# Wider moving operands in a two-block transformer kernel, and another order of its first loads

## The chip, the cores and the metric

The kernel runs on one core of a Trainium2 chip. The metric is the device time of one execution in microseconds; the kernel before takes 840.6 us (median of 3 runs, 839.73 to 841.76).

## What is computed

A sequence of 256 tokens with 1024 channels passes through two blocks in fp32. The parts that matter here:

```python
x = first_block(x, ...)      # even layer (mLSTM + sparse attention), odd layer (gated recurrence)
x = second_block(x, c, ...)  # 2 layers, each: a mixer, then a squared-ReLU MLP

def even_layer(h, w_in, b_in, ...):      # h = rms_norm(x, norm_w[0])
    proj = h @ w_in + b_in               # q, k, v, gates ...
def hgrn2_layer(h, w_in, b_in, ...):     # h = rms_norm(x, norm_w[1])
    fp, iv, qp, z = jnp.split(h @ w_in + b_in, 4, axis=-1)
def sq_relu_mlp(h, w1, w2):              # w1: 1024 x 4096, w2: 4096 x 1024
    return jnp.square(jax.nn.relu(h @ w1)) @ w2
# second_block, layer i
mod = c_act @ ada_w[i] + ada_b[i]        # six 1024-vectors: shifts, scales, gates
x = x + g2[:, None, :] * sq_relu_mlp(modulate(rmsnorm(x, g), sh2, sc2), w1[i], w2[i])
```

## The kernel before, in words

**Numbers.** Each large product is made of fp32r operands in two parts: a value is a rounded high part plus a low rest. A product is the sum of three: high weight by high activation, high weight by low activation, low weight by high activation (L212 to L214 in `mm_T`, L197 to L199 in `tiles_tok`). Each of the three is one TensorE instruction of 128 rows, with its own weight load. Plain fp32 products (norm sums, transposes, attention scores) stand as two records each in the trace.

**Layout.** Activations lie channel-major: 128 channels by 256 tokens, eight such slices. `tile_T` gives 128 output channels: the weight is the loaded operand, the 256 tokens (258 where two columns of the shift are carried along) are streamed. `tiles_tok` gives token-major outputs for v and sv of the even layer and iv of the odd one: 128 tokens of the activation are loaded, 256 columns of the weight are streamed, once for each of the two token halves.

**Weights.** `Weights.piece` loads 1 MB chunks from HBM on SP's queue into three `raw` buffers and splits each half chunk (a piece of 128x1024) by an ACT copy to `whi` (L153) and a DVE subtraction to `wlo` (L154), four buffers each. So a piece costs ACT one cast, DVE one subtraction, and PE 24 products.

**Side work.** The modulation vectors `mod` are formed by DVE (L342) from 96 chunks of 512 KB (`araw`, two buffers, also on SP's queue). A generator hands out this work; `step(n)` places one of its 72 steps (one or two chunks) among other work. SP's queue is in order: an `araw` load that waits for its buffer holds the weight loads behind it.

**Second MLP product.** The 32 slices of the squared ReLU are kept as `ghi` and `glo`, each 128 x 32 x 256. For each of 8 output tiles, 4 pieces of `w2` are taken, and for each of their 8 slices the three products L212 to L214 go into one PSUM bank of 256 columns. `scaled_add` (L321) then adds the tile, times the gate, to `xT`.

**Start.** `prm` (all small parameters, 170 KB, the norm weights among them) is loaded from ACT's queue. SP's queue loads `xT` two slices at a time (256 KB, 2 KB per partition out of rows of 8 KB) and the first weight chunk in three parts (256, 256 and 512 KB, again out of rows of 8 KB), interleaved. `Norm.operand` casts each slice, scaled by the norm weight (ACT L271, DVE L272); `ahead` splits the first piece in two halves; `square` forms the sums for the norm (ACT L277, DVE L280, PE L285). Then the columns of the even layer follow, four tiles before the constants (`cst`, rows) are loaded, the rest after.

The order on each engine is set by a planner that takes the program's order, modelled costs and priorities; PE's order follows the program closely.

Of the kernel before, what the change touches and what calls it, by code (L numbers as in the profile page):

```python
# [8 lines left out]
F32 = mybir.dt.float32  # L9
# [9 lines left out]
T = 256  # L19
# [15 lines left out]
class _Columns:  # L35
# [15 lines left out]
    ("norm_w", 16), ("ev_b", 35), ("f_bias", 1), ("conv_w", 32), ("conv_b", 8),  # L51
# [14 lines left out]
def tile_kernel(ctx: ExitStack, tc: tile.TileContext, io: dict, out: bass.AP):  # L66
# [36 lines left out]
    prm = mk(base, [128, PRM.n], F32, "prm")  # L103
    xT = mk(base, [128, KT, T], F32, "xT")
# [21 lines left out]
    G.memset(ones, 1.0)  # L126
    ident_bf = mk(base, [128, 128], BF16, "identbf")
# [29 lines left out]
    class Weights:  # L157
# [5 lines left out]
        def first(self, c0, c1):  # L163
# [23 lines left out]
    def tiles_tok(w, i, pair, evict):  # L187

        ps = [gbank()[:, :256] for _ in range(2)]
        for half in range(2):  # L190
            wh, wl = w.piece(i + half, 256)
            for tb in range(2):
                ts_ = slice(tb * 128, tb * 128 + 128)
                for k4 in range(4):
                    k = half * 4 + k4
                    st, sp = k == 0, k == KT - 1
                    PE.matmul(ps[tb], pair.hi(k)[:, ts_], wh[:, k4, :], start=st, stop=False)  # L197
                    PE.matmul(ps[tb], pair.lo(k)[:, ts_], wh[:, k4, :], start=False, stop=False)  # L198
                    PE.matmul(ps[tb], pair.hi(k)[:, ts_], wl[:, k4, :], start=False, stop=sp)  # L199
        for tb in range(2):  # L200
            evict(tb, ps[tb])
# [44 lines left out]
    class Norm:  # L246
# [13 lines left out]
        def operand(self, k):  # L260
            if self.pair is None:
                return
            x, p = xT[:, k, :], k // 4
            if self.shift is not None and p not in self.pair.parts:
                hi, lo = [a[:, :, T : T + 2] for a in self.pair.part(p)]
                sh = self.shift[:, 4 * p : 4 * p + 4, None].to_broadcast([128, 4, 2])
                S.copy(hi, sh)
                V.tensor_sub(lo, sh, hi)
            g = self.gain[:, k : k + 1]
            hi, lo = self.pair.hi(k)[:, :T], self.pair.lo(k)[:, :T]  # L270
            S.activation(hi, x, AF.Copy, scale=g)  # L271
            V.scalar_tensor_tensor(lo, x, g, hi, op0=ALU.mult, op1=ALU.subtract)  # L272
# [109 lines left out]
    def even_layer(norm, nxt, w):  # L382
        with ExitStack() as es:
# [13 lines left out]
            V.tensor_tensor(gbias, P("ev_b", b0), P("f_bias"), op=ALU.add)  # L397
            hbias = mk(ev, [128, 35], F32, "hbias")
            V.tensor_scalar(hbias, P("ev_b"), 0.5, None, op0=ALU.mult)
# [51 lines left out]
            def columns(names):  # L451
                for name in names:
                    ti = EV_TILES.index(name)
                    if name in ("v0", "v1", "v2", "v3", "sv0", "sv1"):
                        dst, row = (v, row_v) if name[0] == "v" else (sv, row_sv)
                        c0 = int(name[-1]) * 128
                        if c0 % 256 == 0:
                            tiles_tok(w, ti, pair, lambda tb, ps: V.scalar_tensor_tensor(
                                dst[:, tb, c0 : c0 + 256], ps, rcol[:, tb : tb + 1], row[:, c0 : c0 + 256], op0=ALU.mult, op1=ALU.add))
# [14 lines left out]
            columns(EV_TILES[:4])  # L474
# [5 lines left out]
            columns(EV_TILES[4:11])  # L480
# [296 lines left out]
    def hgrn_layer(norm, nxt):  # L777
        with ExitStack() as es:
# [213 lines left out]
    def mlp(layer, mod, norm, nxt):  # L992
        with ExitStack() as es:
            mp = es.enter_context(tc.tile_pool(name="mp", bufs=1))
            pair = norm.pair
            ghi = mk(mp, [128, 32, T], F32R, "ghi")
            glo = mk(mp, [128, 32, T], F32R, "glo")
            w1 = Weights(lambda c: io["mlp_w1"][layer, c])
            w2 = Weights(lambda c: io["mlp_w2"][layer, c])
            for n in range(32):  # L1000
                if layer == 0 and n % 2 == 0:
                    step(11)
                if layer and n % 4 == 3:
                    step(12)
                if layer == 0 and n == 16:
                    sgu_prepare(*consts)
                ps = gbank()[:, : pair.w]
                tile_T(ps, w1, n, pair)
                r = norm.scaled(ps)
# [4 lines left out]
                S.copy(ghi[:, n, :], r)  # L1014
                V.tensor_sub(glo[:, n, :], r, ghi[:, n, :])
# [110 lines left out]
    n1 = Norm(P("norm_w", 8, 8))  # L1126
# [110 lines left out]
def _pack(inp):  # L1237
# [3 lines left out]
    a["xT"] = np.ascontiguousarray(g["x"][0].T.reshape(KT, 128, T).transpose(1, 0, 2))  # L1241
# [3 lines left out]
    for i, name in enumerate(EV_TILES):  # L1245
        if name not in tok:
            ps.append(_pieces(_take(w, tiles[i]), 8, 128))
        elif name in ("v0", "v2", "sv0"):
            ps.append(_pieces(_take(w, np.concatenate(tiles[i : i + 2])), 4, 256))
    a["ev_w_in"] = _paired(*ps, np.zeros((1, 128, 1024), f))  # L1250
    order = np.concatenate([np.arange(512)] + [512 + np.concatenate([j * 64 + np.arange(64), (j + 4) * 64 + np.arange(64)]) for j in range(4)])
    a["ev_w_out"] = _paired(_pieces(g["ev_w_out"][0][order], 8, 128))
    a["od_w_in"] = _paired(*[_pieces(m, 4 if i == 1 else 8, 256 if i == 1 else 128) for i, m in enumerate(np.split(g["od_w_in"][0], 4, 1))])
# [12 lines left out]
    def per_part(v):  # L1266
# [9 lines left out]
        "norm_w": per_part(g["norm_w"]),  # L1276
# [19 lines left out]
    }  # L1296
    a["prm"] = np.ascontiguousarray(np.concatenate([parts[n].reshape(128, -1) for n in PRM.at], 1))
# [26 lines left out]
```

## Time and profile before

| | |
|---|---|
| median of 3 runs | 840.6 us |
| profiled execution, its own time | 842.29 us |
| its span, first to last instruction | 840.5 us |
| TensorE matmul busy | 810.0 us (96%), 7172 instructions |
| VectorE busy | 667.1 us (79%) |
| ScalarE busy | 516.3 us (61%) |
| DMA | 184.72 MB, mean 220 GB/s |

PE's busy time is the union of overlapping instructions: one 256-column product is shown as 0.28 us, but the next starts 0.12 us after it. What a product takes of PE is the distance between starts, or a window's length divided by the number of products in it.

### The profile page before, as it was taken

Reading aid. Unit: us, or ns where it says so; the run is one execution under the profiler, and the core shown is the slowest. Engines: PE = TensorE matmul, PEld = TensorE weight load, DVE = VectorE, ACT = ScalarE, POOL = GpSimd, SP = SyncE. Lnnn points to the kernel's source line nnn. Section 1 sums busy time; section 2 is a strip of 40 time slices with the busy share of each in tenths; the row PEclk is TensorE's granted clock in tenths of the full one; section 3 lists DMA queues with packets and bytes.
Section 4 is the critical chain, followed back from the end, with each engine's and each line's share of the span. In section 5 each row is a group of like instructions: output and inputs, shape, how many; then the busy total and the mean of one; then the engine's idle time right before and its main releaser. Section 6 shows DMA issues by size and latency. Waiting matters only on the chain.

```text
span 840.5 us, 17614 instructions
## 1 busy us (share of the span) xinstructions
PE 810.0 (96%) x7172; PEld 772.0 (92%) x7172; DVE 667.1 (79%) x1247; ACT 516.3 (61%) x918; POOL 4.9 (1%) x19
## 2 busy tenths in 40 slices
PE   6999999998999999999999998999999999999996
PEld 5989787888998998999999998999999999999995
DVE  7679888899999999999998977756678777754542
ACT  6645656686876565658777633445647777754431
POOL 0000000001000000000000000000000000000000
PEclk9999999999999999999999999999999999999998
DMA  9664266657785777667888888865445454554521
GB/s 328 220 221 171 101 198 218 233 180 265 293 310 201 239 254 282 228 226 246 310 277 289 297 298 295 296 208 194 152 151 185 166 198 161 193 188 168 196 102 50
DMA packets 34497, 184.72 MB, mean 220 GB/s; under 512 B 3825, under 2 KB 4465, under 8 KB 19057
## 3 DMA queue, kind: packets, MB, share of 16 engines
q1 hardware_dynamic: 33984, 182.85, 62.3%
q8 instruction: 56, 0.92, 0.4%
q10 hardware_dynamic: 432, 0.76, 0.3%
q14 instruction: 25, 0.20, 0.1%
HBM read 182.55 MB, written 1.05 MB: 218 GB/s over the span
## 4 chain that ended last, share of the span: by engine, by line
PE 66%; DMA 13%; DVE 10%; ACT 5%; issue 4%; SPq 0%; DVEq 0%; ACTq 0%
PE g L212 17%; PE g L214 17%; PE g L213 16%; DMA araw<-in_ada_w_dram 12%; DVE wlo L154 4%; DVE araw L342 3%; ACT whi L153 1%; PE m L848 1%; PE g L197 1%; PE g L198 1%; PE g L199 1%; PE m L739 1%; PE long L767 1%; PE m L285 1%; DVE nt L301 1%
## 5 line engine op out<-in xcount | busy, mean ns | idle before, releaser
L212 PE MATMUL g<-ahi,whi 128*128 128x258 f32 (+1 forms) x1256 | 359.6, 289 | 10.9 <-ACT whi L153 6.7
L214 PE MATMUL g<-ahi,wlo 128*128 128x258 f32 (+1 forms) x1256 | 356.6, 285 | 3.1 <-DVE wlo L154 3.1
L213 PE MATMUL g<-alo,whi 128*128 128x258 f32 (+1 forms) x1256 | 357.7, 286 | 0.1
L153 ACT CAST whi<-raw 128x1024 fp32r<-128x1024 f32 (+1 forms) x238 | 246.6, 1043 | 168.2 <-PE g L213 134.1
L154 DVE TENSOR_TENSOR wlo<-raw,whi 128x1024 fp32r<-128x1024 f32 (+1 forms) x238 | 289.2, 1217 | 73.7 <-ACT whi L153 73.2
L212 PEld LDWEIGHTS g<-ahi,whi 128*128 128x128 f32 x1256 | 238.3, 190 | 15.6 <-ACT whi L153 6.9
L214 PEld LDWEIGHTS g<-ahi,wlo 128*128 128x128 f32 x1256 | 238.9, 190 | 5.3 <-DVE wlo L154 4.3
L213 PEld LDWEIGHTS g<-alo,whi 128*128 128x128 f32 x1256 | 239.5, 191 | 2.6 <-issue 1.2
L214 PE MATMUL g<-ghi,wlo 128*128 128x256 f32 x512 | 144.5, 282 | 4.5 <-DVE wlo L154 4.4
L213 PE MATMUL g<-glo,whi 128*128 128x256 f32 x512 | 144.7, 283 | 0.0
L212 PE MATMUL g<-ghi,whi 128*128 128x256 f32 x512 | 144.7, 283 | 0.0
L342 DVE CUSTOM_DVE_ANT_0 araw<-araw,row_c,prm 128x1024 f32<-128x1024 f32 x96 | 122.6, 1280 | 25.8 <-DMA araw<-in_ada_w_dram 25.6
L214 PEld LDWEIGHTS g<-ghi,wlo 128*128 128x128 f32 x512 | 96.9, 189 | 5.8 <-DVE wlo L154 5.8
L213 PEld LDWEIGHTS g<-glo,whi 128*128 128x128 f32 x512 | 96.4, 188 | 0.1
L212 PEld LDWEIGHTS g<-ghi,whi 128*128 128x128 f32 x512 | 96.0, 187 | 0.0
L301 DVE TENSOR_TENSOR nt<-g,nrstd 128x256 f32<-128x256 f32 x133 | 55.6, 420 | 21.7 <-PE g L214 21.6
L1012 ACT ACTIVATE nt<-nt,nb 128x256 f32<-128x256 f32 x64 | 32.3, 507 | 19.5 <-DVE nb L1011 19.5
L271 ACT ACTIVATE ahi<-xT,gains 128x256 fp32r<-128x256 f32 x32 | 16.2, 506 | 38.7 <-DVE xT L321 38.0
L197 PE MATMUL g<-whi,ahi 128*128 128x256 f32 x112 | 32.7, 292 | 0.0
L198 PE MATMUL g<-whi,alo 128*128 128x256 f32 x112 | 32.0, 286 | 0.0
L199 PE MATMUL g<-wlo,ahi 128*128 128x256 f32 x112 | 32.0, 286 | 0.0
L277 ACT ACTIVATE sq<-xT 128x256 f32<-128x256 f32 x56 | 22.5, 404 | 12.0 <-DVE xT L321 10.9
(288 smaller groups left out, 824.8 us busy)
## 6 DMA issues: line engine op xcount, KB each, us to landing
raw<-in_mlp_w_dram SPq DMA_DIRECT2D x64, 1024.0 KB, 4.9
araw<-in_ada_w_dram SPq DMA_DIRECT2D x96, 512.0 KB, 5.1
raw<-in_ev_w_in_dram SPq DMA_DIRECT2D x17, 1024.0 KB, 5.4
raw<-in_od_w_in_dram SPq DMA_DIRECT2D x16, 1024.0 KB, 5.6
raw<-in_sgu_w_in_dram SPq DMA_DIRECT2D x8, 1024.0 KB, 4.7
raw<-in_ev_w_out_dram SPq DMA_DIRECT2D x4, 1024.0 KB, 4.9
raw<-in_od_w_out_dram SPq DMA_DIRECT2D x4, 1024.0 KB, 6.0
raw<-in_sgu_w_out_dram SPq DMA_DIRECT2D x4, 1024.0 KB, 4.8
```

Of the source, the lines that this page charges most:

```text
L153: S.copy(hi[:, c], r[:, c])
L154: V.tensor_sub(lo[:, c], r[:, c], hi[:, c])
L197: PE.matmul(ps[tb], pair.hi(k)[:, ts_], wh[:, k4, :], start=st, stop=False)
L198: PE.matmul(ps[tb], pair.lo(k)[:, ts_], wh[:, k4, :], start=False, stop=False)
L199: PE.matmul(ps[tb], pair.hi(k)[:, ts_], wl[:, k4, :], start=False, stop=sp)
L212: PE.matmul(ps, wh(k), ah(k), start=st, stop=False)
L213: PE.matmul(ps, wh(k), al(k), start=False, stop=False)
L214: PE.matmul(ps, wl(k), ah(k), start=False, stop=sp)
L277: S.activation(sq, xT[:, k, :], AF.Square)
L301: V.tensor_tensor(t, ps[:, :T], self.r, op=ALU.mult)
L342: V.tensor_tensor_reduce(raw, raw, crow, 1.0, P("ada_b", layer * 48 + c), ALU.mult, ALU.add, mod[:, c : c + 1])
L1012: S.activation(r, r, AF.Relu, bias=b)
```

## The change

**Token-major products.** `tiles_tok` gets the stream width as an argument. v (four tiles) becomes one call with 512 columns in place of two calls with 256, iv of each half of the heads likewise; sv stays at 256. With 512 columns a piece of the weight holds 2 slices of the contraction, not 4. The host packs the weights accordingly. In `iv_cols` both `step(5)` calls now stand ahead of the one wide call.

**Second MLP product.** `ghi` and `glo` become one tile with the high and the low 256 columns of a slice side by side. The high weight is loaded once and streams all 512 columns; the low weight streams the 256 high ones. The bank then holds two halves; ACT copies the second to SBUF and `scaled_add` runs twice.

**Start.** The norm weights are an array of their own (8 KB), first on ACT's queue, followed there by the first weight chunk in three parts, each contiguous in HBM. `xT` is packed so that each load is contiguous and has SP's queue alone, with `prm` behind it. Nine fp32 products of `ones` by `ones` into a bank that nobody reads stand first on PE. Six column tiles, not four, come before the constants. `gbias` and `hbias`, which read `prm`, are placed on DVE after the last operand.

```diff
-    nc.scalar.dma_start(prm, io["prm"])
+    nc.scalar.dma_start(norm_w, io["norm_w"])
     def load_x(k):
-        nc.sync.dma_start(xT[:, k : k + 2, :], io["xT"][:, k : k + 2, :])
+        nc.sync.dma_start(xT[:, k : k + 2, :], io["xT"][k // 2].rearrange("p (k t) -> p k t", k=2))
+    def warm(n):
+        ps = mbank()
+        for _ in range(n):
+            PE.matmul(ps[:, 0:128], ones, ones, start=True, stop=True)
...
-            nc.sync.dma_start(self.raw[0][:, c0:c1], self.src(0)[:, c0:c1])
+            nc.scalar.dma_start(self.raw[0][:, c0:c1], src)
...
-    def tiles_tok(w, i, pair, evict):
-        ps = [gbank()[:, :256] for _ in range(2)]
-        for half in range(2):
-            wh, wl = w.piece(i + half, 256)
+    def tiles_tok(w, i, pair, n, evict):
+        ps = [gbank()[:, :n] for _ in range(2)]
+        m = 1024 // n
+        for part in range(KT // m):
+            wh, wl = w.piece(i + part, n)
             for tb in range(2):
                 ts_ = slice(tb * 128, tb * 128 + 128)
-                for k4 in range(4):
-                    k = half * 4 + k4
+                for j in range(m):
+                    k = part * m + j
...
-            columns(EV_TILES[:4])
+            columns(EV_TILES[:6])
+            after(V.tensor_tensor(gbias, P("ev_b", b0), P("f_bias"), op=ALU.add), [norm.last])
+            after(V.tensor_scalar(hbias, P("ev_b"), 0.5, None, op0=ALU.mult), [norm.last])
             load_constants()
...
             def iv_cols(h0):
-                for c0 in (h0 * 128, h0 * 128 + 256):
-                    step(5)
-                    tiles_tok(w, 8 + c0 // 128, pair, lambda tb, ps: V.scalar_tensor_tensor(
-                        iv[:, tb, c0 : c0 + 256], ps, rcol[:, tb : tb + 1], row_iv[:, c0 : c0 + 256], op0=ALU.mult, op1=ALU.add))
+                step(5)
+                step(5)
+                c0 = h0 * 128
+                tiles_tok(w, 8 + h0, pair, 512, lambda tb, ps: V.scalar_tensor_tensor(
+                    iv[:, tb, c0 : c0 + 512], ps, rcol[:, tb : tb + 1], row_iv[:, c0 : c0 + 512], op0=ALU.mult, op1=ALU.add))
...
             for n in range(8):
-                ps = gbank()[:, :T]
+                ps = gbank()
                 for c in range(4):
                     wh, wl = w2.piece(4 * n + c, 128)
-                    mm_T(ps, lambda k: wh[:, k, :], lambda k: wl[:, k, :], lambda k: ghi[:, 8 * c + k, :],
-                         lambda k: glo[:, 8 * c + k, :], range(8), first=c == 0, last=c == 3)
+                    for k in range(KT):
+                        a = g[:, 8 * c + k, :, :]
+                        st, sp = c == 0 and k == 0, c == 3 and k == KT - 1
+                        PE.matmul(ps, wh[:, k, :], a.rearrange("p s t -> p (s t)"), start=st, stop=sp, skip_group_check=True)
+                        PE.matmul(ps[:, :T], wl[:, k, :], a[:, 0, :], start=False, stop=sp, skip_group_check=True)
-                scaled_add(mod[:, 40:48])(n, ps)
+                add = scaled_add(mod[:, 40:48])
+                lo = mk(tmp, [128, T], F32, "nt", bufs=3)
+                S.copy(lo, ps[:, T:])
+                add(n, ps[:, :T])
+                add(n, lo)
...
+    w = Weights(lambda c: io["ev_w_in"][c - 1])
+    warm(9)
+    for i in range(4):
+        load_x(2 * i)
+        if i < 2:
+            w.first(512 * i, 512 * i + 512, io["ev_w_0"][i])
+    w.first(1024, 2048, io["ev_w_1"])
+    nc.sync.dma_start(prm, io["prm"])
     tab[0] = Table(EXP_LN)
-    w = Weights(lambda c: io["ev_w_in"][c])
-    load_x(0)
-    w.first(0, 512)
-    load_x(2)
-    w.first(512, 1024)
-    load_x(4)
-    load_x(6)
-    w.first(1024, 2048)
-    n0 = Norm(P("norm_w", 0, 8))
+    n0 = Norm(norm_w[:, 0:8])
```

## Rows read from the trace of the kernel before

**Rows 1.** Page, part 1: busy time, share and instructions of each engine.
```profile
PE 810.0 (96%) x7172; PEld 772.0 (92%) x7172; DVE 667.1 (79%) x1247; ACT 516.3 (61%) x918; POOL 4.9 (1%) x19
```

**Rows 2.** Page, part 5: groups; count, busy us, mean ns, idle before.
```profile
L213 PE MATMUL g<-glo,whi 128*128 128x256 f32 x512 | 144.7, 283 | 0.0
...
L198 PE MATMUL g<-whi,alo 128*128 128x256 f32 x112 | 32.0, 286 | 0.0
```

**Rows 3.** Windows in w2: length, PE, PEld, DVE, ACT, POOL busy (count), clock, DMA, GB/s.
```profile
745.00:815.00 70.00, 70.00 (x586) 70.00 (x585) 34.03 (x35) 30.99 (x37) 0.00 (x0) 1.00 0.48 170
480.00:543.00 63.00, 58.49 (x477) 57.24 (x476) 47.25 (x67) 23.93 (x31) 0.00 (x0) 1.00 0.86 298
550.00:568.00 18.00, 17.99 (x148) 17.72 (x147) 9.11 (x10) 7.01 (x8) 0.00 (x0) 1.00 0.59 204
```

**Rows 4.** Timeline of PE in w2, layer 1: start, length, line, operands.
```profile
740.05 0.28 PE L214 MATMUL g<-ghi,wlo 128*128 128x256 f32 x1
740.18 0.28 PE L212 MATMUL g<-ghi,whi 128*128 128x256 f32 x1
740.29 0.29 PE L213 MATMUL g<-glo,whi 128*128 128x256 f32 x1
```

**Rows 5.** Timeline of PE, plain fp32 streams of 256 and 512 columns.
```profile
359.11 0.59 PE L967 MATMUL m<-raw,mod 128*128 128x256 f32 x2
359.54 0.59 PE L285 MATMUL m<-sq,ones 128*128 128x256 f32 x2
...
143.31 1.02 PE L739 MATMUL m<-kblk,nqk 128*128 128x512 f32 x2
144.17 0.27 PE L740 MATMUL m<-nnegbf,identbf 128*128 128x256 bf16 x1
```

**Rows 6.** Timeline of PE and its weight loads, a transpose behind an fp32r product.
```profile
575.25 0.28 PE L214 MATMUL g<-ahi,wlo 128*128 128x258 f32 x1
575.27 0.25 PEld L1079 LDWEIGHTS m<-cst,vg 128*128 128x128 f32 x2
...
575.37 0.38 PE L1079 MATMUL m<-cst,vg 128*128 128x128 f32 x2
```

**Rows 7.** Timeline of the start, in brackets the idle time before and what ended it.
```profile
0.73 0.41 ACTq L105 DMA_DIRECT2D prm<-in_prm_dram  x1
...
0.80 0.20 POOL L126 MEMSET ones<- 128x128 f32 x1
...
4.93 0.91 ACT L271 ACTIVATE ahi<-xT,prm 128x256 fp32r<-128x256 f32 x2 [2.48 <-DMA prm<-in_prm_dram]
...
8.36 0.41 PE L213 MATMUL g<-alo,whi 128*128 128x256 f32 x1
...
8.57 0.41 PE L214 MATMUL g<-ahi,wlo 128*128 128x256 f32 x1
...
9.74 1.71 ACT L271 ACTIVATE ahi<-xT,prm 128x256 fp32r<-128x256 f32 x4 [0.89 <-DMA xT<-in_xT_dram]
...
11.96 1.03 ACT L153 CAST whi<-raw 128x1024 fp32r<-128x1024 f32 x1
...
14.30 0.58 PE L214 MATMUL g<-ahi,wlo 128*128 128x256 f32 x1 [0.34 <-DVE wlo L154]
```

**Rows 8.** DMA view of the first 16 us: GB/s in 40 slices of 0.4 us.
```profile
GB/s 0 0 0 0 75 162 220 244 182 246 367 394 374 374 338 210 102 118 108 143 251 379 410 435 445 440 471 481 348 410 460 348 444 400 412 340 401 413 430 435
```

**Rows 9.** Waits from 470 to 545 us: total us, times, longest.
```profile
DVE araw L342 <- DMA araw<-in_ada_w_dram: 16.0, 10, 2.4
...
PE g L214 <- DVE wlo L154: 4.4, 4, 2.4
```

**Rows 10.** Window of the iv columns, columns as in rows 3.
```profile
302.40:331.00 28.60, 28.57 (x222) 27.00 (x222) 27.21 (x48) 15.80 (x24) 0.00 (x0) 1.00 0.77 271
```

**Rows 11.** Window at the lower clock, columns as in rows 3.
```profile
87.70:91.10 3.40, 2.81 (x13) 2.82 (x14) 2.85 (x9) 1.40 (x4) 0.10 (x1) 0.50 0.01 2
```

**Rows 12.** Timeline of the end.
```profile
832.12 0.48 DVE L321 SCALAR_TENSOR_TENSOR xT<-g,mod,xT 128x256 f32<-128x256 f32 x1 [9.66 <-PE g L214]
```

More of the change, by code (lines that the diff above doesn't have):

```diff
@@ L161, in __init__, with first @@
             self.src, self.raw, self.split = src, {}, {}
-        def first(self, c0, c1):
+        def first(self, c0, c1, src):
             if not self.raw:
                 self.raw[0] = mk(wpool, [128, 2048], F32, "raw", bufs=3)
-            nc.sync.dma_start(self.raw[0][:, c0:c1], self.src(0)[:, c0:c1])
+            nc.scalar.dma_start(self.raw[0][:, c0:c1], src)
         def ahead(self, i, n):
@@ L185, in tile_T @@
         mm_T(ps, lambda k: wh[:, k, :], lambda k: wl[:, k, :], pair.hi, pair.lo, range(KT))
-    def tiles_tok(w, i, pair, evict):
-        ps = [gbank()[:, :256] for _ in range(2)]
-        for half in range(2):
-            wh, wl = w.piece(i + half, 256)
+    def tiles_tok(w, i, pair, n, evict):
[3 more added lines that the diff above has]
+            wh, wl = w.piece(i + part, n)
             for tb in range(2):
                 ts_ = slice(tb * 128, tb * 128 + 128)
-                for k4 in range(4):
-                    k = half * 4 + k4
+                for j in range(m):
+                    k = part * m + j
                     st, sp = k == 0, k == KT - 1
-                    PE.matmul(ps[tb], pair.hi(k)[:, ts_], wh[:, k4, :], start=st, stop=False)
-                    PE.matmul(ps[tb], pair.lo(k)[:, ts_], wh[:, k4, :], start=False, stop=False)
-                    PE.matmul(ps[tb], pair.hi(k)[:, ts_], wl[:, k4, :], start=False, stop=sp)
+                    PE.matmul(ps[tb], pair.hi(k)[:, ts_], wh[:, j, :], start=st, stop=False)
+                    PE.matmul(ps[tb], pair.lo(k)[:, ts_], wh[:, j, :], start=False, stop=False)
+                    PE.matmul(ps[tb], pair.hi(k)[:, ts_], wl[:, j, :], start=False, stop=sp)
         for tb in range(2):
@@ L271, in operand @@
             S.activation(hi, x, AF.Copy, scale=g)
-            V.scalar_tensor_tensor(lo, x, g, hi, op0=ALU.mult, op1=ALU.subtract)
+            self.last = V.scalar_tensor_tensor(lo, x, g, hi, op0=ALU.mult, op1=ALU.subtract)
         def square(self, k, i=None):
@@ L455, in columns @@
                         dst, row = (v, row_v) if name[0] == "v" else (sv, row_sv)
[L456 to L459, printed above, removed]
+                        if name[-1] == "0":
+                            n = 512 if name[0] == "v" else 256
+                            tiles_tok(w, ti, pair, n, lambda tb, ps: V.scalar_tensor_tensor(
+                                dst[:, tb, :], ps, rcol[:, tb : tb + 1], row, op0=ALU.mult, op1=ALU.add))
                         continue
@@ L479, in even_layer @@
             crow = bcast_rows(base, "c")
-            columns(EV_TILES[4:11])
+            columns(EV_TILES[6:11])
             ns = nsa(ev, et, nqk, sv, gsb, cpair, nout)
@@ L1013, in mlp @@
                 S.activation(r, r, AF.Square)
-                S.copy(ghi[:, n, :], r)
-                V.tensor_sub(glo[:, n, :], r, ghi[:, n, :])
+                split(g[:, n, 0, :], g[:, n, 1, :], r)
             for n in range(8):
-                ps = gbank()[:, :T]
+                ps = gbank()
                 for c in range(4):
@@ L1125, in tile_kernel @@
         n0.square(k)
-    n1 = Norm(P("norm_w", 8, 8))
+    n1 = Norm(norm_w[:, 8:16])
     even_layer(n0, n1, w)
@@ L1240, in _pack @@
     a = {}
-    a["xT"] = np.ascontiguousarray(g["x"][0].T.reshape(KT, 128, T).transpose(1, 0, 2))
+    a["xT"] = np.ascontiguousarray(g["x"][0].T.reshape(4, 2, 128, T).transpose(0, 2, 1, 3)).reshape(4, 128, 2 * T)
     tiles = _ev_columns()
@@ L1247, in _pack @@
             ps.append(_pieces(_take(w, tiles[i]), 8, 128))
-        elif name in ("v0", "v2", "sv0"):
-            ps.append(_pieces(_take(w, np.concatenate(tiles[i : i + 2])), 4, 256))
+        elif name in ("v0", "sv0"):
+            n = 4 if name == "v0" else 2
+            ps.append(_pieces(_take(w, np.concatenate(tiles[i : i + n])), 8 // n, 128 * n))
     a["ev_w_in"] = _paired(*ps, np.zeros((1, 128, 1024), f))
+    first = a["ev_w_in"][0]
+    a["ev_w_0"] = np.ascontiguousarray(first[:, :1024].reshape(128, 2, 512).transpose(1, 0, 2))
+    a["ev_w_1"] = np.ascontiguousarray(first[:, 1024:])
+    a["ev_w_in"] = np.ascontiguousarray(a["ev_w_in"][1:])
     order = np.concatenate([np.arange(512)] + [512 + np.concatenate([j * 64 + np.arange(64), (j + 4) * 64 + np.arange(64)]) for j in range(4)])
     a["ev_w_out"] = _paired(_pieces(g["ev_w_out"][0][order], 8, 128))
-    a["od_w_in"] = _paired(*[_pieces(m, 4 if i == 1 else 8, 256 if i == 1 else 128) for i, m in enumerate(np.split(g["od_w_in"][0], 4, 1))])
+    a["od_w_in"] = _paired(*[_pieces(m, 2 if i == 1 else 8, 512 if i == 1 else 128) for i, m in enumerate(np.split(g["od_w_in"][0], 4, 1))])
     a["od_w_out"] = _paired(_pieces(g["od_w_out"][0], 8, 128))
@@ L1275, in _pack @@
     parts = {
-        "norm_w": per_part(g["norm_w"]),
         "ev_b": ev_b,
@@ L1296, in _pack @@
     }
+    a["norm_w"] = np.ascontiguousarray(per_part(g["norm_w"]))
     a["prm"] = np.ascontiguousarray(np.concatenate([parts[n].reshape(128, -1) for n in PRM.at], 1))
```

8 lines of the change are left out of this document (3 added, 5 removed).

## The prediction

> **What bounds the kernel now.** Read the engines' busy times first: PE 96%, DVE 79%, ACT 61% [rows 1]. So the question for each edit is whether it shortens the row of products on PE. A busy share does not say how fast PE streams, so the next view is windows inside one stage: in the second MLP product of layer 1, 586 products start in 70.00 us, one every 0.1195 us, at the full clock [rows 3]. [...] DVE (34 of 70 us) and ACT (31 of 70 us) are half idle there: PE alone sets this stage. In layer 0 the same work takes 63 us for 477 products, 0.132 us each, with DMA at 0.86; the rest of the stage is back at 18.00/148 = 0.122 [rows 3]. There a second limit acts: DVE waits 16.0 us for `araw` in ten waits, and PE 4.4 us for `wlo` behind it [rows 9].
>
> [...] The timeline shows distances of 0.13 and 0.11 in turn with equal column counts [rows 4], so it isn't a plain rate per column. Is it the weight load? Behind an fp32r product a transpose has a shorter kind of load (0.25 us for two, overlapped), begun at once, and still its stream starts 0.12 us after the product before [rows 6]. So the stream itself holds PE for 0.12 us. [...]
>
> **Second MLP product.** 8 tiles x 4 pieces x 8 slices = 256 steps per layer, each three products of 256 columns; after, one of 512 and one of 256. The 768 columns stay, one product goes. Bounds for the 512-column stream: above, twice 0.1195 = 0.239 (the extra is per column): nothing gained. [...]
>
> [...]
>
> Layer 1 has ACT and DVE to spare, so all 3.3 us count. In layer 0 five of the eight tiles (477 of 768 products) lie in the stretch with the second limit. Six stall-microseconds stand there (63 - 477 x 0.1195); a faster PE partly just waits longer for `wlo`. I count the last three tiles in full (1.25 us) and a third of the first five (0.7): 2.0 us, bounds 0 and 5.9.
>
> Added: one ACT copy out of PSUM and one more `scaled_add` of 0.48 us [rows 12] per tile. Seven of eight lie beside PE's next tile (96 products, 11 us). The last one of layer 1 stands on the path to the final norm: after PE's last product comes L321 at 832.12, then the square; now a second L321 comes between. The ACT copy runs beside the first. Cost 0.5 us. The last tile of layer 0 feeds the next layer's operand of slice 7, which is needed after 21 products (2.5 us), so its 0.5 us is hidden; uncovered it would cost 0.5.
>
> **Token-major products.** v: 96 products of 256 become 48 of 512; iv: 192 become 96. [...] In the stretch of iv DVE is busy 27.2 of 28.6 us [rows 10]: a faster PE meets DVE almost at once, so I take 1.0 for iv, 1.6 together. The evictions move the same elements in half as many instructions. Two `step(5)` in a row put two to four `araw` loads on SP's queue before the next weight load; two `raw` chunks loaded ahead (two pieces each, 2.9 us a piece) cover about 11 us of it. Without the cover see the fourth rival.
>
> **Start.** The first product starts at 6.40 us, a step late in a chain on ACT: idle 2.48 us until `prm` lands at 4.93, then casts, then 0.89 us idle for `xT`, and the second piece's cast ends at 11.96 + 1.03 = 12.99; its low part releases PE at 14.30 [rows 7]. From 4.93 to 12.99 are 8.1 us, in which the needed work is eight operand casts (1.71/4 = 0.43 each, 3.4) and two pieces (1.03 and, in halves, some 1.2): 5.7. So 2.4 us are waits, and squares that filled them. The DMA row says why: around 6.4 to 8.0 us it moves 102 to 143 GB/s, against 350 to 480 from 8.4 us on [rows 8]; at 0.4 MB per us the 6.0 to 8.4 us stretch (0.37 MB) would have taken 0.9 us, 1.5 less. The loads then in flight are those out of 8 KB rows. With contiguous sources, and `xT` before `prm`, I let those waits go. The first operands need 0.5 MB, not 0.67 with `prm`: by the sums of [rows 8] 4.1 in place of 4.6 us, 0.4 less. Together at most 2.8 us; I take 2.2, since squares still have to run somewhere.
>
> [...]
>
> The ones products: nine, as plain fp32 two records each. [...] They may bring the upper level earlier. The first 24 products are held by their operands either way (24 x 0.21 = 5.1 us against 5 us of casts), so this is worth 0.09 us for each of the few products behind them: 0.4, bound 1.0. Start in all 2.6 (bounds 0, if the loads stay as slow, and 3.8). ACT's three more issues of 0.41 us lie in its 2.48 us idle time. Six tiles before the constants, not four, delay nothing that PE's order needs in the first 25 us: nothing.
>
> **Sum.** 2.6 + 1.6 + 2.0 + 3.3 - 0.5 = 9.0 us. The profiled execution took 842.3 (span 840.5 and 1.8 around it), 1.7 above the median of 840.6; against it the sum gives 833.3, and against the median 831.6.
>
> **Rivals.**
> [...]
> [...]
> *The start stays.* The slow spell is not from the sources' layout: 9.0 - 2.6 = 6.4, 834.2 us.
> *SP's queue, slower.* The `araw` loads that now stand together, ahead of iv, hold the weight loads, and the faster MLP of layer 0 meets them as well. Price: the longest such wait so far is 2.4 us [rows 9], and a stretch of 3.4 us at the lower clock, as seen after an idle PE at 87.7 us [rows 11], costs another 1.7: 4.1 each. It decides from the third on (9.0/4.1 = 2.2); with three 840.6 - 9.0 + 12.3 = 843.9. Against it: in iv's stretch PE has no such idle time now [rows 10].
>
> **Numbers.** Chances: forecast 0.43, per column 0.24, all hidden 0.15, start stays 0.10, SP's queue 0.08. The range is 824 to 839.5: it holds the first four cases and leaves out the queue and some of the edges, two in ten. A measurement of this kernel tells about 0.2% (1.7 us) from no change, so faster means under 838.9. The per-column case lies at that edge; I give it half to each: faster 0.80, same 0.12, slower 0.08.
>
> **What would show it.** [...] Layer 1's stage goes from 92 to 88.5 us. At the start: the second piece's `wlo` product near 12 us, not 14.30, and no slow spell in the GB/s row. In layer 0: DVE's waits for `araw`. The prediction is wrong if PE stands still in iv's stretch, or the first data product starts later than 6.4 us.

## The result, and the profile after

| | before | after |
|---|---|---|
| median, us | 840.16 (4 runs, 837.74 to 841.76) | 829.66 (4 runs, 829.24 to 830.74) |
| profiled execution, its span, us | 842.29, 840.5 | 830.03, 828.2 |

The ratio is 0.9879, with a 95% interval of 0.9853 to 0.9906: 10.2 us less by that ratio, 7.9 to 12.4 (gains below are told by their ratios too, which can differ by a microsecond from the difference of the medians). In a later set beside other runs of before, the same kernel took 827.83 us, ratio 0.9857 (0.9831 to 0.9882).

PE's busy time, in the page's first part, hardly moved, though 638 records fewer stand there than in [rows 1]: 656 matmul instructions went, 18 records of the ones products came.

```profile
PE 807.2 (97%) x6534; PEld 740.2 (89%) x6534; DVE 672.1 (81%) x1257; ACT 520.3 (63%) x934; POOL 4.9 (1%) x19
```

Windows of the kernel after (columns as in [rows 3]): the second MLP product of layer 1, its first and last tiles in layer 0, and the stretch of iv, which answers to [rows 10].

```profile
735.00:800.00 65.00, 65.00 (x373) 56.81 (x372) 35.22 (x40) 30.44 (x42) 0.00 (x0) 1.00 0.51 178
470.00:533.00 63.00, 60.34 (x340) 51.65 (x339) 51.60 (x74) 26.69 (x38) 0.00 (x0) 1.00 0.89 310
536.00:556.00 20.00, 20.00 (x114) 17.22 (x113) 16.07 (x21) 9.11 (x14) 0.00 (x0) 1.00 0.74 260
296.27:324.90 28.63, 28.63 (x131) 22.82 (x130) 26.04 (x43) 16.47 (x25) 0.00 (x0) 1.00 0.75 258
```

In layer 1 there are 373 records in 65 us, so some 0.349 us for a pair of 512 and 256 columns (0.350 by the distances below), where three products at [rows 3] took 0.3585 by the same count (0.3596 by their distances, 119.9 ns each: the count takes in products under way at the window's start). PE is still never idle there; in layer 0 it idles 2.7 of 63 us. PE's timeline in layer 1, which answers to [rows 4]:

```profile
759.98 0.39 PE L1035 MATMUL g<-ghl,whi 128*128 128x512 f32 x1
760.22 0.28 PE L1036 MATMUL g<-ghl,wlo 128*128 128x256 f32 x1
760.34 0.39 PE L1035 MATMUL g<-ghl,whi 128*128 128x512 f32 x1
760.57 0.28 PE L1036 MATMUL g<-ghl,wlo 128*128 128x256 f32 x1
```

A 512-column stream is followed after 0.231 or 0.234 us, mean 232.5 ns over 199; the 256-column product after 117.5. The two waits of layer 0's stage that answer to [rows 9] (total, times, longest) are shorter in total, not gone:

```profile
DVE araw L351 <- DMA araw<-in_ada_w_dram: 12.0, 10, 2.8
...
PE g L1036 <- DVE wlo L162: 2.4, 2, 1.4
```

The timeline of the start, beside [rows 7]:

```profile
1.05 4.21 PE L133 MATMUL m<-ones 128*128 128x128 f32 x18 [1.05 <-POOL ones L127]
...
4.10 0.91 ACT L280 ACTIVATE ahi<-xT,norm_w 128x256 fp32r<-128x256 f32 x2 [0.20 <-DMA norm_w<-in_norm_w_dram]
...
5.90 0.58 PE L221 MATMUL g<-ahi,whi 128*128 128x256 f32 x1 [0.64 <-ACT whi L161]
...
7.30 0.62 ACT L161 CAST whi<-raw 128x512 fp32r<-128x512 f32 x1 [1.45 <-DMA raw<-in_ev_w_dram]
...
10.11 0.41 PE L223 MATMUL g<-ahi,wlo 128*128 128x256 f32 x1
10.32 0.41 PE L221 MATMUL g<-ahi,whi 128*128 128x256 f32 x1
...
11.15 1.03 ACT L161 CAST whi<-raw 128x1024 fp32r<-128x1024 f32 x1
...
13.49 0.38 PE L223 MATMUL g<-ahi,wlo 128*128 128x256 f32 x1
```

The slow spell of [rows 8] is gone; the DMA view of the first 16 us:

```profile
GB/s 0 0 0 0 77 83 305 342 356 404 410 405 364 369 343 353 384 384 415 368 482 475 405 389 492 430 369 492 410 389 451 430 364 446 368 427 352 327 166 143
```

ACT's first cast comes 0.83 us earlier, the first product 0.5; ACT then waits 1.45 us for the second half of the first weights. From 9.69 us on, products stand 0.21 us apart without idle time: PE at that pace (0.12 us from 13.7 us on) is the bound there, not the casts.

At the end, DVE has two additions where [rows 12] had one:

```profile
819.29 0.48 DVE L330 SCALAR_TENSOR_TENSOR xT<-g,mod,xT 128x256 f32<-128x256 f32 x1 [8.20 <-ACT nt L1041]
819.81 0.48 DVE L330 SCALAR_TENSOR_TENSOR xT<-nt,mod,xT 128x256 f32<-128x256 f32 x1
```

Where the profiled 12.3 us went, stage by stage. A stage runs from the first product of its kind to the first of the next; the first score product of the odd layer's attention is called the odd layer's start below.

| stage, by PE's first products | before | after | difference |
|---|---|---|---|
| to the 240th 256-column product (a 512 counts as two) | 43.12 | 40.14 | -2.98 |
| from there to the odd layer's attention | 198.23 | 196.25 | -1.98 |
| to the second MLP product, layer 0 | 228.72 | 227.66 | -1.06 |
| that product, layer 0 | 98.92 | 94.20 | -4.72 |
| to layer 1's second MLP product | 170.11 | 170.24 | +0.13 |
| that product, layer 1, first to last start | 92.71 | 90.08 | -2.62 |
| to the final norm's sum | 1.62 | 2.55 | +0.93 |

These are single executions. Only the last three rows repeat from run to run (to 0.2 us); the experiments show what the others are made of.

### The profile page after: what moved, and what is told of

It reads as the page before. It is cut to its first block, busy times and chain, and to the rows that moved or that the text cites. A ratio compares the mean times of both kernels' runs of the same rounds, so it can differ in the third digit from the quotient of the medians.

```text
span 828.2 us, 16357 instructions
## 1 busy us (share of the span) xinstructions
PE 807.2 (97%) x6534; PEld 740.2 (89%) x6534; DVE 672.1 (81%) x1257; ACT 520.3 (63%) x934; POOL 4.9 (1%) x19
## 4 chain that ended last, share of the span: by engine, by line
PE 66%; DMA 13%; DVE 12%; ACT 5%; issue 4%; DVEq 0%; ACTq 0%; SPq 0%
PE g L221 12%; PE g L222 12%; DMA araw<-in_ada_w_dram 12%; PE g L223 12%; PE g L1035 9%; PE g L1036 5%; DVE wlo L162 4%; DVE araw L351 3%; ACT whi L161 2%; PE g L207 1%; PE g L208 1%; PE g L206 1%; PE m L858 1%; PE m L748 1%; PE long L776 1%
## 5 line engine op out<-in xcount | busy, mean ns | idle before, releaser
L1035 PE MATMUL g<-ghl,whi 128*128 128x512 f32 x512 | 179.9, 394 | 0.6 <-DVE nb L1020 0.6
L1036 PE MATMUL g<-ghl,wlo 128*128 128x256 f32 x512 | 143.5, 280 | 2.7 <-DVE wlo L162 2.4
L1035 PEld LDWEIGHTS g<-ghl,whi 128*128 128x128 f32 x512 | 96.0, 187 | 23.3 <-issue 0.7
L1036 PEld LDWEIGHTS g<-ghl,wlo 128*128 128x128 f32 x512 | 96.0, 187 | 4.0 <-DVE wlo L162 3.9
L214 DVE TENSOR_TENSOR ghl<-nt,ghl 128x256 fp32r<-128x256 f32 x64 | 27.0, 423 | 3.8 <-ACT ghl L213 1.4
L1022 ACT ACTIVATE nt<-nt 128x256 f32<-128x256 f32 x64 | 26.7, 418 | 1.9
L213 ACT CAST ghl<-nt 128x256 fp32r<-128x256 f32 x64 | 25.9, 406 | 1.9
L208 PE MATMUL g<-wlo,ahi 128*128 128x512 f32 (+1 forms) x64 | 24.3, 379 | 0.0
L206 PE MATMUL g<-whi,ahi 128*128 128x512 f32 (+1 forms) x64 | 24.2, 378 | 0.0
```

Source lines behind the costliest of these rows:

```text
L206: PE.matmul(ps[tb], pair.hi(k)[:, ts_], wh[:, j, :], start=st, stop=False)
L208: PE.matmul(ps[tb], pair.hi(k)[:, ts_], wl[:, j, :], start=False, stop=sp)
L1035: PE.matmul(ps, wh[:, k, :], a.rearrange("p s t -> p (s t)"), start=st, stop=sp, skip_group_check=True)
L1036: PE.matmul(ps[:, :T], wl[:, k, :], a[:, 0, :], start=False, stop=sp, skip_group_check=True)
```

## Experiments

**One part of the change at a time, and the change without its ones products.** Four kernels in one set, before taking 841.22 us.

The MLP edit alone:

```diff
-                    mm_T(ps, lambda k: wh[:, k, :], ..., lambda k: ghi[:, 8 * c + k, :], ...)
+                        PE.matmul(ps, wh[:, k, :], a.rearrange("p s t -> p (s t)"), ...)
+                        PE.matmul(ps[:, :T], wl[:, k, :], a[:, 0, :], ...)
```

> The kernel before with the second MLP product alone changed (512-column stream and its split eviction). In the kernel after, a step of 512 + 256 columns takes 0.3495 us against 0.36 us for three products before, 10 ns x 256 = 2.7 us per layer; yet layer 0's stage became 4.7 us shorter and layer 1's 1.7. Theory A (layer 0 gains twice: a shorter stream, and fewer stalls on weight splits because PE and the other engines drift less apart, and that belongs to this edit alone): 6.4 us, some 834 us, with layer 0's stage near 94.2 us, as after. Rival B (layer 0's second part came from the start and the token-major edits, which shift the phase of its loads): layer 0 gives about 2.7, layer 1 1.7, together 4.4, some 836 us, layer 0's stage at 96 us or more. Rival C (the stated forecast, a fixed extra per stream): 512-column distance 0.226, 4.8 us in all, 3.3 - 0.5 of them in layer 1.

Measured: 832.29 us, ratio 0.9883 (0.9856 to 0.9910): 9.8 us by the ratio, 7.6 to 12.1 (8.9 by the medians). Layer 1 gave its 2.61 us and took 1.02 back at the end. Layer 0's stage took 90.76 us, 8.2 less, PE waiting 0.4 us in it. B and C fall. A's amount was too small: this run's layer 0 had even fewer waits than the first profile of the kernel after.

The start alone:

```diff
-    nc.scalar.dma_start(prm, io["prm"])
+    nc.scalar.dma_start(norm_w, io["norm_w"])
...
+    warm(9)
...
-            columns(EV_TILES[:4])
+            columns(EV_TILES[:6])
```

> The kernel before with the start alone changed (contiguous first loads, norm weights apart, nine products of ones, six tiles ahead of the constants, gbias and hbias later). Theory A: products are about 1.4 us ahead at the end of the first four tiles and, since a later wait of 1 us for a weight's low part goes too, 2.5 to 3 us ahead from the tenth tile on, and this stays to the end: 837.6 us. Rival B (the even layer's attention part gives it back, since DVE sets it): products ahead by 3 us at 50 us, by less than 1 us at the start of the odd layer; 840 us. Rival C (the start is worth more than its own window, because the attention part then meets its loads in a better order; in the kernel after, the odd layer starts 5.0 us earlier): 836 us.

Measured: 836.95 us, ratio 0.9943 (0.9921 to 0.9965): 4.8 us, 2.9 to 6.6. The 240th product is 3.9 us ahead, the odd layer's start 5.1: nothing is given back, B falls. C is the nearer one, though the interval holds A too.

The token-major products alone:

```diff
-    def tiles_tok(w, i, pair, evict):
+    def tiles_tok(w, i, pair, n, evict):
```

> The kernel before with the token-major products alone changed (v and iv at 512 columns). In the kernel after, a 512-column token-major stream takes 231 to 234 ns against 2 x 119.5: 5 to 8 ns x 144 = 0.7 to 1.2 us in all. Theory A (DVE sets iv's stretch, so its part is lost, and only v's 0.3 us counts): 840.3 us, iv's stretch as long as before within 0.3 us. Rival B (all of the stream's gain counts): 839.6 us. Rival C (two steps of side work in a row hold the weight loads): iv's stretch longer by 1 us or more, 842 us.

Measured: 840.31 us, ratio 0.9993 (0.9974 to 1.0012). The interval ends at 842.2 us, so none of the three can be excluded by the time. In the profile the stretch from the last score product to the last product with iv took 30.33 us (before 29.14), as C said, but PE waits 0.7 us in it for DVE's `hiv`, not for weights. The distances say what is to be had: in the kernel before token-major products stood 118.5 ns apart (pauses left out), so 2 x 118.5 - 232 = 5 ns x 144, 0.7 us.

The three gains add up to 15.2 us, more than the 10.2 of the whole: 5 us, at an uncertainty of about 4. Something seems to be counted twice, and the profiles say what: layer 0's stage took 90.76, 95.20 and 97.00 us in these three, 8.2, 3.7 and 1.9 less than before, 13.8 together, where without any wait it has only 8.6 to lose (98.9 to 90.3). Besides, the profile of the MLP edit alone has no stretch at the lower clock (0.50) between the start and the end, that of the kernel after has two of 3.4 us.

```diff
-    warm(9)
```

> The kernel after without the nine products of ones (their result is read by nothing). In the kernel after the granted clock rises at 13.37 us, before at 16.03. Theory A (the ones products bring the rise forward): without them it rises near 16 us again; products in these 2.7 us stand 0.213 us apart in place of 0.12, so 9 to 10 fewer are done: 1.1 us lost, 830.8 us. Rival B (the rise belongs to the data products, which start 0.5 us earlier and have fewer gaps): rise at 13.4 us still, 829.7 us. Rival C (they stand in the way of the first product): first product earlier than 5.90 us, time below 829.4.

Measured: 832.66 us, ratio 0.9893 (0.9862 to 0.9924), not told apart from the kernel after. The clock rose at 13.31 us (13.37 in the kernel after), in this pair as B said (other profiles with the ones products rise earlier, see the last section); the first product came at 5.70, 0.2 earlier, as C said, and nothing came of it. What no theory named: the order written out by the planner is another from 44 us on. A product of the attention part, in the kernel after,

```profile
49.36 1.12 PE L621 MATMUL m<-nqk,cst 128*128 128x512 f32 x2
```

and without the ones products, where it comes behind another stretch of v:

```profile
55.54 1.08 PE L621 MATMUL m<-nqk,cst 128*128 128x512 f32 x2
```

From the 240th product to the odd layer this run took 200.12 us, the kernel after 196.25, each with two low-clock stretches of 3.4 us. But the profiled execution, at 837.60 us, was the slowest of this kernel's six (829.16 to 837.60). So the order differs, and whether that difference costs anything is not shown.

**The second layer's modulation loads taken away, in both kernels.**

```diff
-                        nc.sync.dma_start(raw, io["ada_w"][layer, c])
-                        V.tensor_tensor_reduce(raw, raw, crow, 1.0, ...)
+                        if layer == 0:
+                            nc.sync.dma_start(raw, io["ada_w"][layer, c])
+                        V.tensor_tensor_reduce(raw, raw if layer == 0 else crow, crow, 1.0 if layer == 0 else 1e-3, ...)
```

> The kernel after without the loads of the second layer's modulation chunks: DVE's 48 reductions of layer 1 read a resident row in their place, so its work stays and 25 MB of transfers and the waits for araw go (layer 1's modulation is then not the reference's). In the kernel after, layer 0's stage of the second MLP product takes 94.2 us, 4.1 more than layer 1's 90.1 with the same products. Theory A (the difference is the wait of the weights' low part behind DVE's wait for araw): layer 0's stage falls to 90.1 to 90.5, the time by some 4 us or a little more (first MLP product unchanged) to 825.5. Rival B (DVE's own work sets it, 78 of 94 us busy): the stage stays near 94, time 829.5. Rival C (the whole side work costs in other places too): time below 823.

> The kernel before, with the same loads left out. Its layer-0 stage takes 98.9 us against 92.7 in layer 1. Theory A (the 6.2 us are waits behind araw, which any change of pace can shorten): the stage falls to 92.7 to 93.2 and the time by about 6 us to 834.5; the difference to the changed kernel without the loads is then what the streams, the start and the token-major products give by themselves, 2.6 + 1.7 + 2.5 + 0.5 = 7.3 us, less than the 10.2 measured between the two kernels with them. Rival B (the waits are not what made the changed kernel faster in layer 0): the difference stays at 10 us or more.

Measured: 824.85 us and 835.65 us, beside 839.63 of before. Layer 0's stage as one window, first the changed kernel, then the one before:

```profile
461.35:551.64 90.29, 90.29 (x517) 78.54 (x516) 69.98 (x98) 42.01 (x56) 0.00 (x0) 1.00 0.56 194
```

```profile
468.71:561.58 92.87, 92.85 (x773) 92.59 (x772) 66.01 (x89) 40.28 (x49) 0.00 (x0) 1.00 0.53 186
```

PE is busy for the whole window, and both stages are as long as layer 1's. A fits the stage in both kernels: what exceeds 90.3 (or 92.9) us would be the chain from the `araw` load over DVE to the weight's low part. For the old product the evidence is fair: with the loads its stage took 98.9, 97.0 (3.4 us of it at the lower clock) and 95.2 us in three profiles. For the new one it is thin, since a profile with the loads also has 90.29 (the repeat below). With the waits away the edit is worth 2.57 us in layer 0, as in layer 1.

But A's time for the pair was wrong, and rival B right: the two still lie 10.8 us apart (about 2.4 either way), not 7.3. The stages of the two profiles, 11.5 us apart in span, place it: 2.7 to the 240th product, 1.7 more to the odd layer, 3.0 from there to the MLP of layer 0, 2.6 and 2.6 in the two MLP products, less 0.9 at the end. Of the 3.0, 2.3 are waits of PE at the odd layer's attention (L849, L910) which the changed kernel did not have in that run; the kernel after has 0.9 of such waits in one profile and 1.9 in another, so that part moves between executions.

**Low products last, and the last tile as before.**

```diff
+                    if layer and n == 7:
+                        mm_T(ps[:, :T], ...)          # three 256-column products
+                        continue
+                    for k in range(KT):
+                        PE.matmul(ps, wh[:, k, :], a(k).rearrange("p s t -> p (s t)"), ...)
+                    for k in range(KT):
+                        PE.matmul(ps[:, :T], wl[:, k, :], a(k)[:, 0, :], ...)
```

> The kernel after, with two edits in the second MLP product: of each piece the eight 512-column products come first and the eight with the low weight after them, so that a late low part has 1.9 us more; and the last tile of layer 1 takes the three 256-column products again, so that the end has one addition. Theory A (layer 0's excess is waits for the low part, longest 1.4 us): layer 0's stage falls from 94.2 to about 91, the end by 0.9 - 0.3 = 0.6 us, together 3.5 us, 826 us. Rival B (DVE is late by its mean rate, so a later need only moves the wait): layer 0 within 1 us of 94, time 829. Rival C (two 512-column streams in a row, each with its own weight, take more than 232 ns each): layer 1's stage longer than 90.1 by several tenths or more.

Measured: 827.21 us, ratio 0.9849 (0.9828 to 0.9869). Waits for the low part are gone from layer 0, where one other wait of 1.6 us remains (L294, the norm's sum), and the stage took 92.83 us. That the edit removed them is not shown: the repeat below has none without it, at 827.83 us. C's sign came too: layer 1's products took 91.26 us, 0.75 more than with the same last tile and the usual order (90.51, further below), 3.3 ns for each of 224 steps. Only part of it is C's: 512-column streams in a row stand 233.8 ns apart (232.4 in the usual order), 256-column ones 119.8 (117.5).

**A third buffer for araw, throughout.**

```diff
-                        raw = mk(wpool, [128, 1024], F32, "araw", bufs=2)
+                        raw = mk(wpool, [128, 1024], F32, "araw", bufs=3)
```

> The kernel after with three buffers for araw in place of two, so that a load is issued one reduction earlier. Theory A (the wait for araw is the time from a freed buffer to the landing): DVE's waits for araw in layer 0's second MLP product fall from 12.0 us by half or more, the stage from 94.2 to 91 to 92, the time by 2 us or more to 827.5. Rival B (the loads share the DMA engines with the weights, 298 GB/s there, and come no sooner): waits as before, 829.7. Rival C (the earlier araw loads hold the weight loads on SP's queue): ACT waits for raw longer than its 11.2 us, time 831 or more.

Measured: 829.18 us, ratio 0.9872 (0.9853 to 0.9891). The wait for `araw` fell to 4.7 us and layer 0's stage to 90.28, below A's 91 to 92; the time did not follow. The odd layer starts at 239.96 us, 3.6 later than in the kernel after: the attention part is in another order and stands 13.7 us at the lower clock (0.50), the kernel after 6.8.

**Other widths.**

```diff
+                    w1_ = T * 2 if layer == 0 else 512 - 64 * (n // 2)
+                    w2_ = T if layer else 256 - 64 * (n // 2)
...
+                        PE.matmul(ps[:, :w1_], wh[:, k, :], a[:, :w1_], ...)
+                        PE.matmul(ps[:, :w2_], wl[:, k, :], a[:, :w2_], ...)
```

> The kernel after with other stream widths in the second MLP product, two output tiles each. Layer 1: 512, 448, 384 and 320 columns for the high weight (the low activation's last columns are left out, and its addition where fewer than 512 are streamed), 256 for the low weight. Layer 0: 512 for the high weight, and 256, 192, 128 and 64 for the low one (part of that product is left out). Read from the distances between starts at the full clock; in the kernel after they are 232.5 ns for 512 columns and 117.5 for 256. Theory A (a rate per column and almost nothing fixed: the line through these two is 2.5 ns + 0.449 ns per column): 448: 204, 384: 175, 320: 146; 192: 89, 128: 60. [...] A narrow stream bounded by its weight load would show one distance from some width down.

Measured in one execution, as mean distances in ns at the full clock (1.00), the longer ones at pauses left out: 512 columns 232, 448: 203.4, 384: 175.7, 320: 147.6. A narrow product is followed after 88.5 (192 columns), 59 (128) and 28 ns (64). All agree with A's line of 2.5 ns + 0.449 ns per column to 1.5 ns or better, but for the 64-column one, which lies 3 below. The four widest alone lie on 0.439 ns per column with 7 ns fixed, so the split between the two is known to some 5 ns only. PE's timeline at 448 and at 384 columns, and with a low product of 64:

```profile
780.14 0.37 PE L1037 MATMUL g<-ghl,whi 128*128 128x448 f32 x1
780.35 0.28 PE L1038 MATMUL g<-ghl,wlo 128*128 128x256 f32 x1
...
800.10 0.34 PE L1037 MATMUL g<-ghl,whi 128*128 128x384 f32 x1
800.28 0.28 PE L1038 MATMUL g<-ghl,wlo 128*128 128x256 f32 x1
...
556.00 0.47 PE L1037 MATMUL g<-ghl,whi 128*128 128x512 f32 x1
556.31 0.19 PE L1038 MATMUL g<-ghl,wlo 128*128 128x64 f32 x1
556.34 0.47 PE L1037 MATMUL g<-ghl,whi 128*128 128x512 f32 x1
```

The last three show something else: with 64 columns in place of 256 a pair still takes 0.34 us. Of the 90 ns that the narrow product saves, the 512-column one takes 80 back (312 in place of 232). The weight load for the next wide product starts together with the narrow one, at 556.31 us:

```profile
556.31 0.19 PEld L1037 LDWEIGHTS g<-ghl,whi 128*128 128x128 f32 x1
```

**A version from the above, the kernel after again, and the third buffer alone.** One set, before taking 840.72 us.

```diff
+                        raw = mk(wpool, [128, 1024], F32, "araw1" if layer and c % 3 == 2 else "araw", bufs=1 if layer and c % 3 == 2 else 2)
...
+                        if layer and n == 7:
+                            mm_T(ps[:, :T], ..., [k], first=st, last=sp)
```

> The kernel after with a third buffer for the second layer's araw chunks (every third chunk of that layer has its own) and the three 256-column products for layer 1's last tile. Theory A (the two gains stand beside each other): layer 0's stage 90.3 us in place of 94.2, as with three buffers throughout; the end 1.6 us in place of 2.5, for 0.3 us more of products: together 4.5 us, 825 to 826 us. Rival B (the third buffer shifts the attention part's order, as it did with three buffers throughout, and gives back 2 to 3 us there): 828 us.

> The kernel after once more, unchanged, beside the others on the same chip. Theory A (layer 0's waits for the low part vary from execution to execution): layer 0's stage between 90.3 and 96 us and not 94.2 again, layer 1's 90.1 and the end 2.55 again to 0.02 us. Rival B (they are fixed by the kernel): 94.2 to 0.3 us again. Time 829.7.

Measured: 827.58 us (0.9850, 0.9826 to 0.9873) and 827.83 us (0.9857, 0.9831 to 0.9882): no difference to be told. The end is 0.93 us shorter for 0.42 us of products. Layer 0's stage took 90.29 us in both, so the third buffer had nothing left to take. A's 825 to 826 us were not reached; with the third buffer the odd layer starts at 239.18 us, 1.8 later than in the repeat, as B had it. The kernel after again, as one window:

```profile
465.74:556.03 90.29, 90.29 (x517) 78.54 (x515) 75.33 (x108) 42.40 (x59) 0.00 (x0) 1.00 0.86 307
```

The same kernel had 94.20 us in its first profile. So theory A of the repeat holds: the waits of layer 0 vary between executions, and the 2.1 us by which that stage gained more than its stream in the first pair of profiles are no property of the edit that one execution could show.

The kernel before with the third buffer alone, the edit as above with 3 in place of 2:

> The kernel before with three buffers for araw and nothing else changed. Theory A (layer 0's excess over 92.7 us is the wait for araw in both kernels, and a third buffer takes it away): layer 0's stage falls from 98.9 to some 92.8, the time by 4 to 6 us to 835.5, about half of what the whole change gives, with no wider stream. Rival B (before, the slower streams leave the loads more time, so a third buffer gives less): stage 96 or more, 838 or more.

Measured: 841.97 us, ratio 1.0006 (0.9985 to 1.0027). Layer 0's stage fell to 92.86 us, 6.1 less, as A said (other profiles of the same product with two buffers have 95.2 and 97.0, so the buffer's share is 2.3 to 6.1), and the whole gained nothing: A's time was wrong, and B's 838 or more came without its mechanism. The windows show where it went: the attention part from the 240th product to the first of L728, and its two stretches at the lower clock.

```profile
43.13:146.79 103.66, 96.23 (x664) 79.73 (x663) 83.37 (x197) 56.17 (x131) 1.14 (x7) 0.92 0.52 174
117.30:124.10 6.80, 5.98 (x22) 3.92 (x22) 4.28 (x13) 2.95 (x10) 0.00 (x0) 0.50 0.78 256
131.00:141.10 10.10, 10.10 (x40) 7.58 (x39) 3.02 (x9) 2.12 (x6) 0.00 (x0) 0.50 0.60 203
```

To the same product (L729 there) with two buffers and no such stretch, in the kernel before without the modulation loads:

```profile
43.15:140.92 97.77, 94.43 (x715) 80.53 (x714) 84.00 (x197) 58.79 (x135) 1.13 (x7) 1.00 0.52 177
```

5.9 us longer, with 51 PE records fewer in it, and the odd layer starts 7.9 us later than in the kernel before. The attention part comes in another order, with waits of 1.3, 0.8 and 2.0 us at L579 and L557 near those stretches. In the two stretches PE was busy for 16.1 us at 0.50; fp32r products take 0.21 us there and 0.12 at the full clock, so some 7 us, most of the loss, are the clock's (an estimate from these rows). The other executions say the same: the mean granted clock of this kernel's twelve is 0.985 to 0.993, that of 17 of the kernel before 0.990 to 0.998, and the two with the highest clock (0.993 and 0.991) are the fastest, 836.17 and 838.30 us. That speaks for a gain of the buffer which the lower clock takes back; that the new order lowers the clock is likely, and which of its moves does was not tried.

## Why the prediction came out right, and where its steps did not

The forecast of 831.6 us lies 1.9 above the measured median, by terms of which several were off, in both directions. What it priced measured some 2.5 (start) + 0.7 (token-major) + 2.6 + 2.6 (the two layers' streams) - 0.9 (end) = 7.5 us; the other 2.7 of the 10.2 are waits in layer 0 and the attention part, for which it had no price or too small a one. That the sum met the time is in part luck.

**Fixed extra per product: wrong.** No run shows the fixed extra that stands behind the 3.3, 2.0 and 1.6 us of the sum and behind the 0.226 us taken for a 512-column stream. The stream takes 0.2325, and the widths show why: 128, 192, 256, 320, 384, 448 and 512 columns take 59, 88.5, 117.5, 147.6, 175.7, 203.4 and 232 ns. That is 0.44 to 0.45 ns for each column, and only 2.5 to 7 ns are fixed. It is the per-column case, nearly at the upper bound of 0.239. But that bound's price, nothing gained, was wrong too, because 0.1195 (119.9 ns by the distances: of the 586 products in [rows 3] 583 start in the window) was not the length of a stream but the mean in a row of three: beside a 512-column one the 256-column product takes 117.5 ns. The pair takes 350 where three took 360; by the line of 2.5 and 0.449 ns, some 2.4 ns go on each of three products, and 2.5 fixed ns with the one left out. The layer gave 2.6 us, not 3.3. The reason why [rows 4] alternate was not settled.

**Layer 0: sized too low.** Its stream gave the same 2.6 us; counting a third of the first five tiles was the wrong way to take the second limit. That limit is not a share: it is waits on top of PE's own time (4.4 us for low parts before, 2.4 in the first profile of the kernel after, none in its second), and whether an execution meets them varies. The forecast of 2.0 lay within what single pairs of runs give.

**Start: 2.6 forecast, 2.5 found by the 240th product, and some 1.7 more that was not seen.** That product comes at 39.2 to 40.9 us in nine profiles with the new start and at 42.2 to 43.2 in five with the old, 2.5 apart on average (2.7 and 3.0 in the two pairs above). The loads did what was said: no slow spell. Whether the layout of the sources did it is not shown, since queue and order changed with it and no run takes them apart. But "the second piece's low product near 12 us" failed, it came at 13.49: with the operands earlier, PE at 0.21 us per product became the bound. By the 96th product only 1.4 us are gained in the first pair; the rest comes behind it, where among others a wait of 0.76 us for a low part at 26 us is gone. The further 1.7 us (195.2 against 196.9 from the 240th product to the odd layer, in the pair without modulation loads and without low-clock stretches) lie in the attention part, for which the prediction had priced nothing. That its order makes them is not shown; kernels with the new start took 195.2 to 200.1 us there.

**Token-major: 1.6 forecast, 0.7 to be had by the distances, not resolved by a time.** The step that failed is the same fixed extra. PE never stood still in iv's stretch, and DVE, at 26.0 of 28.6 us, was near its limit, as said. From the last score product of that layer's attention to the last product with iv it took 29.14 us before and 28.94 after.

**End: 0.5 forecast, 0.93 found.** The ACT copy does not run beside the first addition, which waits for it ("8.20 <-ACT nt L1041" in its row): 0.4 us, and the second addition adds 0.5.

**Ones products: free, but without a gain by the clock.** They took 4.21 us and ended at 5.26, ahead of the first product at 5.90. The 0.4 us for an earlier upper level did not appear in the run without them.

**Of the rivals**, SP's queue did not set the time, but part of it is there: in layer 0's stage ACT's waits for weight chunks grew from 4.7 to 11.2 us, the longest from 2.1 to 3.3, while the longest `araw` wait is 2.8 us and PE waited 2.4 us for low parts in all. "Start stays" falls with the start alone. "All hidden" falls with the pair, which takes 350 ns, 10 less than the three products.

## What to carry to other kernels

Take the distance of a product from the pattern in which it will stand, not from the one it leaves: in a mixed row the same 256 columns took 2 ns less (117.5 for 119.9). Where side work shares DVE and the DMA engines with the weights, read an excess over PE's own time as waits that come and go, and test with the loads left out; a second profile of the same kernel moved that stage by 3.9 us. In a kernel whose order a planner writes, compare the order and the granted clock first: with one more buffer a stage was 6 us shorter, and the time came back in another that stood 17 us at the lower clock (0.50).

## What the runs showed of the hardware

- Streams of fp32r took 0.453 to 0.461 ns per column in all at the granted clock of 1.00 (232 ns for 512 columns to 147.6 for 320); a record of plain fp32 took 0.84 ns per column, 0.215 us for 256 and 0.430 for 512 [rows 5]. In the stretches at 0.50 of both kernels (87.7 to 91.1 us before, 74.8 to 78.2 after) 256 fp32r columns took 0.213 us.
- A narrow product did not pay between wide ones with another weight: with 256, 192, 128 and 64 columns the pair took 350, 346, 343 and 340 ns. The last leaves 340 - 232 = 108 ns beside the wide stream. The load of the next wide product's weight starts only with the narrow stream, as its row at 556.31 us shows (0.19 us long, the wide stream follows at 556.34); that this load makes the 108 ns is an estimate, no run takes it apart.
- The clock's first rise, where products go from 0.213 to 0.12 us apart (13.37 us in the profile of the kernel after, 16.03 before): with the ones products it came at 4.5 to 6.0 us in five of eight profiles and fell again between 7.9 and 12.7 us, after products had waited for operands (0.83 and 0.76 us in the repeat, 0.21 us apart from 12.96 us on); in three it came at 13.4 to 14.1. Without them it came at 11.7 to 16.0 us in six profiles, and did not fall back before 84 us. By the 96th product all lay within 22.8 to 24.2 us but for the start alone (21.9).
- The clock also fell with PE never waiting over 0.15 us in the 24 us before (the kernel after at 74.81 us), and PE was busy for all of the stretch that followed:

```profile
74.80:78.20 3.40, 3.40 (x18) 3.31 (x17) 3.40 (x9) 2.40 (x7) 0.20 (x2) 0.50 0.59 183
```
